# Routing eight experts from the raw residual: the router's product moved into the projection before it, and the first expert gathered alone

## The chip, the cores and the metric

The kernel runs as one program on one core of a Trainium2 chip. The metric is device time in microseconds, from the first to the last instruction and what little lies around it; of several executions the median is given. The core has a matrix engine (TensorE, "PE" in the rows, its weight loads "PEld"), a vector engine (VectorE, "DVE"), an activation engine (ScalarE, "ACT"), a general engine (GpSimd, "POOL") and a queue engine (SyncE, "SP") that issues most transfers. Matrix products land in PSUM, which has eight banks of 512 float32 columns.

## The reference, cut to what matters

Two blocks run one after the other on 256 tokens of width 1024, in float32. The last two parts of the second block matter here: a Fourier mixing layer with an output projection, which adds to the residual `x`, and a mixture of eight experts of which every token takes two.

```
x = x + gate * (fourier(norm1(x)) @ w_o + b_o)
h = rms_norm(x, norm2_g) * (1 + scale) + shift        # the experts' input
logits = h @ router                                    # (256, 8)
top_v, top_i = top_k(logits, 2)
gates = softmax(top_v)
for every token, for its two experts e:
    x += gate2 * gates[e] * ((silu(h @ w1[e]) * (h @ w3[e])) @ w2[e])
out = rms_norm(x, final_g)
```

## The kernel before, in words

**The ring of weights.** All weights come over one queue (SP) in units of 1 MB, each into a slot of a ring (`raw_unit`, line 123). In the experts' stage the ring has 16 slots: ten in the pool `ringB`, which the stages before also use, and six in `ringC`, whose memory only comes free when the Fourier projection is over. A unit is asked for as soon as the slot before it is released by the last product that reads it.

**The projection before.** `out_proj` takes `w_o` in two halves of two units. For each half it walks over two token halves `tt` and two column blocks `u`; each of these is 24 products, then two VectorE operations (lines 397 and 398) that add the result into `x`, and a ScalarE square with a sum (line 320) for the next norm. TensorE's order here is made by a planner that goes by readiness and program order.

**From the projection to the first expert.** `row_rstd` sums the squares and makes the inverse root in some ten tiny VectorE operations (lines 335 and 176 to 183). `norm_T` scales and transposes `x` in one product with a diagonal (line 363) and applies scale and shift while it copies out of PSUM, one half of a bank on VectorE (line 366), the other on ScalarE (line 368), into `mhT`. The router's product (line 1061) gives logits as rows; they are transposed, each token's two experts are found (lines 1070 to 1091), positions in each expert's list follow from two products with a triangle and with ones (1096, 1097) and three VectorE operations, and `rank_experts` sorts the experts by load. Position 0 is always expert 0, whatever its load. `mhT` is transposed back to rows `ht` (lines 1108 and 1110).

**Gather.** `gather` builds for a pair of experts a one-hot matrix from tokens to slots (line 1227) and multiplies it with `ht` (line 1234), which gives the pair's inputs, features on the partitions, in `xg`. It does so in four steps; each fills one bank with two blocks of 192 columns and copies both out in one ScalarE copy (line 1236). The first pair is gathered before the first expert. Later pairs are gathered in the last chunk of an odd expert: a step is queued as a filler and issued after each fourth of an `expert_up` half.

**The experts.** `experts_in_order` fixes TensorE's order by hand. Each expert runs seven chunks; a chunk needs six units: four for `expert_up` (w1 and w3, two halves), two for `expert_down` of the chunk before. The number of slots of 32 tokens per place is `PLACE_STRIPS = (3, 2, 3, 3, 2, 3, 3, 2)`, and TensorE's work is in proportion to it, while the bytes are the same for all.

Of the kernel before, what the change touches and what calls it, by code (L numbers as in the profile page):

```python
# [9 lines left out]
F = mybir.dt.float32  # L10
# [3 lines left out]
AF = mybir.ActivationFunctionType  # L14
OP = mybir.AluOpType
# [4 lines left out]
T = 256  # L20
KD = D // 128
# [78 lines left out]
class Kern:  # L100
# [281 lines left out]
    def out_proj(self, pool, w, yhi, ylo, targets):  # L382
# [616 lines left out]
    def fourier(self):  # L999
        nc, a, x = self.nc, self.a, self.x  # L1000
        with ExitStack() as st:
# [33 lines left out]
            self.out_proj(A, a["fnet_w_o_2"][0], fh, fl, [(self.X, g, 0)])  # L1035

    def moe(self):
        nc, tc, a, x, ct, sm = self.nc, self.tc, self.a, self.x, self.ct, self.sm
        with ExitStack() as st:
            A = self.pool(st, "MA", 1)  # L1040
            ht = A.tile([128, 2, D], F, name="ht")
            G = A.tile([128, 2, N_EXP], F, name="G")
            pos = A.tile([128, 2, N_EXP], F, name="pos")
            later = [A.tile([128, 2, N_EXP], F, name="pos%d" % i) for i in (2, 3, 4)]
            cnt = A.tile([128, 1], I32, name="cnt")
            order = A.tile([128, N_EXP], I32, name="order")
            with ExitStack() as s2:
                ps_all = self.pool(s2, "mps1", 2, psum=True)
                self.ps = ps_all
                N = self.pool(s2, "MN", 1)  # L1050
                g2 = self.gate("g_a1_2")
                hT = N.tile([128, KD, 256], F, name="mhT", bufs=1)
                rw = N.tile([128, KD, N_EXP], F, name="rw", bufs=1)
                nc.gpsimd.dma_start(rw, a["moe_router_2"][0].rearrange("(k p) e -> p k e", p=128))
                self.norm_T(N, self.X, *self.scale_cols(self.need("a1_2"), 0, self.vec["norm2"][:, 8:16]), dst_f=hT)
# [3 lines left out]
                lg = ps_all.tile([128, 512], F, tag="mm", name="mm")  # L1059
                for k in range(KD):  # L1060
                    nc.tensor.matmul(lg[0:N_EXP, :T], rw[:, k, :], hT[:, k, :], start=k == 0, stop=k == KD - 1)
                lT = N.tile([N_EXP, T], F, name="lT", bufs=1)
                nc.vector.tensor_copy(lT, lg[0:N_EXP, :T])
                lt = ps_all.tile([128, 512], F, tag="mm", name="mm")
                for tt in range(2):
                    nc.tensor.transpose(lt[:, N_EXP * tt:N_EXP * tt + N_EXP], lT[:, 128 * tt:128 * tt + 128],
                                        self.id[0:N_EXP, 0:N_EXP])
                for tt in range(2):
                    ls = sm.tile([128, N_EXP], F, tag="ls", name="ls")
                    nc.vector.tensor_copy(ls, lt[:, N_EXP * tt:N_EXP * tt + N_EXP])  # L1070
# [5 lines left out]
                    nc.vector.tensor_copy(tf, ti)  # L1076
                    e = sm.tile([128, 1], F, tag="ge", name="ge")
# [6 lines left out]
                    m1 = sm.tile([128, 8], F, tag="m1", name="m1")  # L1084
                    m2 = sm.tile([128, 8], F, tag="m2", name="m2")
                    io = ct[:, C_IO8:C_IO8 + 8]
                    nc.vector.tensor_scalar(m1, io, tf[:, 0:1], None, OP.is_equal)
                    nc.vector.tensor_scalar(m2, io, tf[:, 1:2], None, OP.is_equal)
                    nc.vector.tensor_add(M[:, tt, :], m1, m2)
# [3 lines left out]
                off = N.tile([128, 2, N_EXP], F, name="off")  # L1093
                nc.vector.tensor_scalar(off, M.bitcast(F), -1000.0, 1000.0, OP.mult, OP.add)
                pp = ps_all.tile([128, 2, 2, N_EXP], F, tag="mm", name="mm")
                nc.tensor.matmul(pp[:, 0], tri, M, start=True, stop=True)
                nc.tensor.matmul(pp[:, 1], self.ones_r, M, start=True, stop=True)
                sums = N.tile([128, 2, N_EXP], F, name="sums")
                nc.vector.tensor_copy(sums, pp[:, 1])
                nc.vector.tensor_add(pos, off, pp[:, 0])  # L1100
                nc.vector.tensor_add(pos[:, 1, :], pos[:, 1, :], sums[:, 0, :])
                nc.vector.tensor_add(sums[:, 0, :], sums[:, 0, :], sums[:, 1, :])
                self.rank_experts(N, sums[:, 0, :], pos, G, order, cnt, later)
                for tt in range(2):
                    for j in range(2):
                        tp = ps_all.tile([128, 512], F, tag="tp", name="tp")
                        for b in range(4):
                            nc.tensor.transpose(tp[:, 128 * b:128 * b + 128], hT[:, 4 * j + b, 128 * tt:128 * tt + 128], self.id)
                        js = slice(512 * j, 512 * j + 512)
                        (nc.scalar.copy, nc.vector.tensor_copy)[j](ht[:, tt, js], tp)  # L1110
# [3 lines left out]
            nc.gpsimd.tensor_scalar(self.wfin, self.wfin, -0.125, 0.0, OP.mult, OP.add)  # L1114
            self.B = self.pool(st, "MB", 2)
            more = self.pool(st, "ringC", 1)
# [3 lines left out]
            self.mh = dict(ht=ht, G=G, g2=g2, order=order)  # L1120
            self.experts(pos)
# [5 lines left out]
    def rank_experts(self, N, n, pos, G, order, cnt, later):  # L1127
# [23 lines left out]
        old = N.tile([128, 2, N_EXP], F, name="old")  # L1151
        for v in (pos, G):
            nc.vector.tensor_copy(old, v)
            for tt in range(2):
                turn(v[:, tt, :], old[:, tt, :])
        for i, p in enumerate(later):
            for tt in range(2):
                nc.vector.scalar_tensor_tensor(p[:, tt, :], cap, -float(i + 1), pos[:, tt, :], op0=OP.mult, op1=OP.add)
# [6 lines left out]
    def experts(self, pos):  # L1165

        with self.tc.manual_schedule(engines={mybir.EngineType.PE}):
            self.experts_in_order(pos)

    def experts_in_order(self, pos):  # L1170
        nch = D_FF // 512
        self.fill = []
        pairs = [None, None]
        self.gather(0, pos, pairs)
        self.filler(99)
        prev = None
        for e in range(N_EXP):
            for c in range(nch):
                if c == 0:
                    s = dict(e=e, id=self.expert_id(e), n=PLACE_STRIPS[e], **pairs[e % 2])  # L1180
# [38 lines left out]
    def gather(self, e0, pos, pairs):  # L1219

        nc, ct, B, ps, ht = self.nc, self.ct, self.B, self.mp, self.mh["ht"]
        iota = ct[:, C_IOTA:C_IOTA + SLOTS]
        n = 2 * SLOTS
        oh = B.tile([128, 2, 2, SLOTS], F, tag="oh", name="oh")
        for tt in range(2):
            for i in range(2):
                nc.vector.tensor_scalar(oh[:, tt, i, :], iota, pos[:, tt, e0 + i:e0 + i + 1], None, OP.is_equal)
        xg = B.tile([128, KD, n], F, tag="xg", name="xg")

        def step(k):  # L1230
            g = ps.tile([128, 512], F, tag="sc", name="sc", bufs=1)
            for i in range(2):
                for tt in range(2):
                    nc.tensor.matmul(g[:, n * i:n * i + n], ht[:, tt, 128 * (k + i):128 * (k + i) + 128],
                                     oh[:, tt].rearrange("p i s -> p (i s)"), start=tt == 0, stop=tt == 1)
            nc.scalar.copy(xg[:, k:k + 2, :], g[:, :2 * n].rearrange("p (k s) -> p k s", k=2))

        for k in range(0, KD, 2):
            self.fill.append(lambda k=k: step(k))
        for i in range(2):  # L1240
            pairs[i] = dict(oh=oh[:, :, i, :], xg=xg[:, :, SLOTS * i:SLOTS * i + SLOTS])
# [174 lines left out]
    def run(self):  # L1416
# [18 lines left out]
        with ExitStack() as st:  # L1435
            self.gp = self.pool(st, "gates2", 3)
            self.ring, self.ring_n = self.pool(st, "ringB", 2), (RING, 4, 4, 2048)
            self.rings, self.ring_at = [(self.ring, RING)], 0
            with ExitStack() as s2:
                self.hl = self.pool(s2, "halves", 2)  # L1440
                self.dense_ffn()
                self.ps = self.pool(s2, "ps3", 2, psum=True)
                self.fourier()
            self.moe()
# [33 lines left out]
```

## Time and profile before

| | |
|---|---|
| timed executions | 2065.04, 2073.06, 2074.27 us; median 2073.06 |
| the profiled execution | 2067.9 us, of which the span is 2065.8 |
| TensorE busy | 1945.0 us (94%) |
| VectorE busy | 814.2 us (39%) |
| ScalarE busy | 584.6 us (28%) |
| mean transfer rate over the span | 262 GB/s |

A busy time is a sum over the whole span. Matrix products are pipelined, so a busy TensorE may still wait inside. A float32 product appears as two records, a transpose as one.

### The profile page before, as it was taken

The numbers are of one execution on the slowest core, as the hardware profiler recorded it, in microseconds if no ns is written. First come the engines' busy times: TensorE is split into PE (matmuls) and PEld (weight loads), VectorE is DVE, ScalarE is ACT, GpSimd is POOL, SyncE is SP. The second block draws the span as 40 slices with busy tenths as digits, with TensorE's granted clock in tenths as the row PEclk, the third lists the DMA queues.
The fourth block names the chain that finished last, engine by engine and source line by source line (L and its number), as shares of the span: only waits on it lengthen the run. The fifth ranks groups of instructions, "written<-read, shape, count | busy, mean of one in ns | idle before, by whom it ended". The sixth has DMA issues, their size and how long they took to land. (4 is left out here: it accounts for less than half of the span.)

```text
span 2065.8 us, 49872 instructions
## 1 busy us (share of the span) xinstructions
PE 1945.0 (94%) x21993; PEld 1377.4 (67%) x21993; DVE 814.2 (39%) x2008; ACT 584.6 (28%) x1191; POOL 34.4 (2%) x43
## 2 busy tenths in 40 slices
PE   6999999988999987999979799999999989999995
PEld 3896469954889667999968565555556545655552
DVE  4794676876755475555554201110110101010112
ACT  3334463444623453444442101010101101010101
POOL 1000000000000000000021000000000000000000
PEclk9999999999999988999989899999999999999998
DMA  9567613574245504755553499999999999999995
GB/s 366 206 204 249 227 39 115 158 266 165 74 165 184 198 18 157 251 184 184 185 175 115 172 383 390 392 393 393 390 388 388 387 394 389 389 389 389 389 392 200
DMA packets 249956, 541.77 MB, mean 262 GB/s; under 512 B 9926, under 2 KB 88524, under 8 KB 241540
## 3 DMA queue, kind: packets, MB, share of 16 engines
q1 hardware_dynamic: 248448, 537.12, 71.5%
q8 instruction: 174, 2.85, 0.6%
q0 software_dynamic: 1040, 0.84, 0.3%
q10 hardware_dynamic: 244, 0.55, 0.1%
q14 instruction: 50, 0.41, 0.1%
HBM read 537.38 MB, written 1.10 MB: 261 GB/s over the span
## 5 line engine op out<-in xcount | busy, mean ns | idle before, releaser
L1265 PE MATMUL ha<-raw,xg 128*32 128x256 f32 x7168 | 461.5, 382 | 15.7 <-DMA raw<-in_moe_w_dram 15.7
L1265 PEld LDWEIGHTS ha<-raw,xg 128*32 128x32 f32 x7168 | 226.1, 110 | 184.7 <-issue 23.3
L1290 DVE TENSOR_TENSOR es<-es,ha 64x512 f32<-64x512 f32 x56 | 38.7, 691 | 670.6 <-ACT es L1289 670.6
L141 DVE TENSOR_TENSOR lo<-raw,hi 128x1024 fp32r<-128x1024 f32 (+2 forms) x176 | 214.6, 1226 | 178.6 <-ACT hi L140 178.2
L140 ACT CAST hi<-raw 128x1024 fp32r<-128x1024 f32 (+2 forms) x180 | 187.7, 1051 | 183.0 <-PE acc L153 65.8
L1265 PE MATMUL ya<-raw,gt 128*32 128x256 f32 x3584 | 224.1, 379 | 1.3 <-DMA raw<-in_moe_w_dram 0.6
L1265 PE MATMUL hb<-raw,xg 128*32 128x256 f32 x2240 | 176.6, 380 | 0.0
L1265 PEld LDWEIGHTS ya<-raw,gt 128*32 128x32 f32 x3584 | 117.3, 110 | 78.2 <-DMA raw<-in_moe_w_dram 1.5
L1300 ACT COPY gt<-tp 128x384 f32<-128x384 f32 (+1 forms) x56 | 24.6, 439 | 408.7 <-PE tp L1298 400.4
L151 PE MATMUL h<-fhh,hi 128*128 128x256 f32 x448 | 124.2, 285 | 0.9 <-ACT h L368 0.9
L152 PE MATMUL h<-fhl,hi 128*128 128x256 f32 x448 | 124.3, 285 | 0.0
L153 PE MATMUL h<-fhh,lo 128*128 128x256 f32 x448 | 122.6, 285 | 0.0
L1265 PEld LDWEIGHTS hb<-raw,xg 128*32 128x32 f32 x2240 | 74.6, 110 | 48.7 <-issue 0.6
L1289 ACT ACTIVATE es<-ha 64x512 f32<-64x512 f32 x56 | 33.0, 589 | 254.3 <-PE ha L1265 254.3
L151 PE MATMUL mm<-hi,dhh 128*128 128x256 f32 x320 | 90.3, 283 | 0.0
L153 PE MATMUL mm<-hi,dhl 128*128 128x256 f32 x320 | 89.8, 281 | 0.0
L152 PE MATMUL mm<-lo,dhh 128*128 128x256 f32 x320 | 89.4, 280 | 0.0
L261 PE MATMUL modps<-mraw,s 128*32 128x512 f32 x512 | 78.8, 610 | 10.7 <-DMA mraw<-in_ada_w_dram 10.7
L151 PEld LDWEIGHTS h<-fhh,hi 128*128 128x128 f32 x448 | 85.9, 194 | 2.7 <-ACT h L368 1.2
L152 PEld LDWEIGHTS h<-fhl,hi 128*128 128x128 f32 x448 | 86.0, 194 | 0.9
L1265 PE MATMUL yb<-raw,gt 128*32 128x256 f32 x1120 | 86.1, 379 | 0.0
L153 PEld LDWEIGHTS h<-fhh,lo 128*128 128x128 f32 x448 | 85.0, 194 | 0.7
(434 smaller groups left out, 3415.8 us busy)
## 6 DMA issues: line engine op xcount, KB each, us to landing
raw<-in_moe_w_dram SPq DMA_DIRECT2D x336, 1024.0 KB
mraw<-in_ada_w_dram SPq DMA_DIRECT2D x48, 1024.0 KB
raw<-in_ff_w_dram SPq DMA_DIRECT2D x42, 1024.0 KB
raw<-in_w_in_dram SPq DMA_DIRECT2D x14, 1024.0 KB
raw<-in_attn_w_qkv_dram SPq DMA_DIRECT2D x12, 1024.0 KB
m<-in_w_mod_dram SPq DMA_DIRECT2D x8, 1024.0 KB
mraw<-in_w_mod_dram SPq DMA_DIRECT2D x16, 512.0 KB
mraw<-in_w_mod_dram SPq DMA_DIRECT2D x8, 1024.0 KB
```

Of the source, the lines that this page charges most:

```text
L140: nc.scalar.copy(hi[:, :n], v)
L141: eng.tensor_sub(lo[:, :n], v, hi[:, :n].bitcast(F))
L151: mm(ps, lh, rh, start=first, stop=False)
L152: mm(ps, lh, rl, start=False, stop=False)
L153: mm(ps, ll, rh, start=False, stop=last)
L261: nc.tensor.matmul(ps[32 * j:32 * j + 32, :], stat[:, k, :], raw[:, 512 * j:512 * j + 512], start=k == 0, stop=k == KD - 1)
L1265: self.nc.tensor.matmul(out[32 * q:32 * q + 32, :], x(t), w, start=first and t != 1, stop=last, skip_group_check=True)
L1289: nc.scalar.activation(v, b[0:64, :c1 - c0], AF.Silu)
L1290: nc.vector.tensor_mul(v, v, b[64:128, :c1 - c0])
L1300: nc.scalar.copy(g.rearrange("p b h s -> p (b h s)")[:, :128 * n], t[:, :128 * n])
```

## The change

The router's product is taken from `x` itself. With `a` and `b` the columns of scale and shift, `h = x * rstd * a + b`, so the logits are `rstd * (x @ (a * router)) + b @ router`. `router_begin` loads the router's weights on GpSimd's queue ahead of the projection and prepares `a * router` and `b @ router`. After each half of `out_proj`, `router_part` transposes that half's columns of `x`, copies them out of PSUM and multiplies them with `a * router` into two banks of their own. After the projection, the logits are one VectorE operation per token half. The rows that are gathered are now `x * rstd` (one ScalarE operation per token half); scale and shift are applied when a gathered block is copied out of PSUM, so each feature block has a copy of its own. The first expert is gathered alone, with a one-hot matrix made before the ranking, and the others as pairs (1, 2), (3, 4), (5, 6) and 7 alone, in the last chunk of an even expert. The ranking writes into new tiles. `ringC` is opened ahead of the other pools, on the ground where the halves of the projection's weights lay.

```diff
     def out_proj(self, pool, w, yhi, ylo, targets, after=None):
...
+            if after:
+                after(u0)
...
+            self.router_begin()
+            self.out_proj(A, a["fnet_w_o_2"][0], fh, fl, [(self.X, g, 0)], self.router_part)
+
+    def router_begin(self):
...
+        nc.gpsimd.dma_start(rw, a["moe_router_2"][0].rearrange("(k p) e -> p k e", p=128))
+        self.rt_ab = self.scale_cols(self.need("a1_2"), 0, self.vec["norm2"][:, 8:16])
...
+        nc.vector.tensor_mul(self.rwa, rw, ac[:, :, None].to_broadcast(shape))
...
+        nc.tensor.matmul(ps[:, :N_EXP], self.ones, sb, start=True, stop=True)
...
+    def router_part(self, u0):
+
+        nc = self.nc
+        for u in (u0, u0 + 1):
+            tp = self.ps.tile([128, 2, 256], F, tag="tp", name="tp")
+            for t in range(2):
+                for i in range(2):
+                    k = 2 * u + i
+                    nc.tensor.transpose(tp[:, i, 128 * t:128 * t + 128], self.x[:, t, 128 * k:128 * k + 128], self.id)
+            for t in range(2):
+                ts = slice(128 * t, 128 * t + 128)
+                (nc.vector.tensor_copy, nc.scalar.copy)[t](self.xT[:, 2 * u:2 * u + 2, ts], tp[:, :, ts])
+                for k in (2 * u, 2 * u + 1):
+                    nc.tensor.matmul(self.lg[t][:, :N_EXP], self.xT[:, k, ts], self.rwa[:, k, :],
+                                     start=k == 0, stop=k == KD - 1)
...
+            more = self.pool(st, "ringC", 1)
             A = self.pool(st, "MA", 1)
...
-                self.norm_T(N, self.X, *self.scale_cols(self.need("a1_2"), 0, self.vec["norm2"][:, 8:16]), dst_f=hT)
...
+                rs = [self.row_rstd(self.X, tt) for tt in range(2)]
+                es = []
                 for tt in range(2):
                     ls = sm.tile([128, N_EXP], F, tag="ls", name="ls")
-                    nc.vector.tensor_copy(ls, lt[:, N_EXP * tt:N_EXP * tt + N_EXP])
+                    nc.vector.scalar_tensor_tensor(ls, self.lg[tt][:, :N_EXP], rs[tt], self.lb, op0=OP.mult, op1=OP.add)
+                    nc.scalar.activation(ht[:, tt, :], x[:, tt, :], AF.Copy, scale=rs[tt])
...
+                first = self.onehot(A, "first", pos, 0, 1)
...
+                self.rank_experts(N, sums[:, 0, :], (pos, posp), (G, Gp), order, cnt, later)
-                for tt in range(2):
-                    for j in range(2):
-                        tp = ps_all.tile([128, 512], F, tag="tp", name="tp")
...
-        self.gather(0, pos, pairs)
+        self.gather(0, 1, pos, pairs, first)
...
-                if c == nch - 1 and e % 2 and e + 1 < N_EXP:
-                    self.gather(e + 1, pos, pairs)
+                if c == nch - 1 and e % 2 == 0 and e + 1 < N_EXP:
+                    self.gather(e + 1, min(2, N_EXP - 1 - e), pos, pairs)
...
+        kn = 4 if begin else 2
+
+        def step(k0):
+            g = self.mp.tile([128, 512], F, tag="h%s" % "ab"[k0 // 4] if begin else "sc", name="sc", bufs=2 if begin else 1)
+            for i in range(kn):
                 for tt in range(2):
...
+                k, v = k0 + i, g[:, n * i:n * i + n]
+                if begin and i % 2:
+                    nc.vector.tensor_scalar(xg[:, k, :], v, ac[:, k:k + 1], bc[:, k:k + 1], OP.mult, OP.add)
+                else:
+                    nc.scalar.activation(xg[:, k, :], v, AF.Identity, bias=bc[:, k:k + 1], scale=ac[:, k:k + 1])
```

## Rows read from the trace of the kernel before

**Rows 1.** Stretches: length; PE, PEld, DVE, ACT, POOL busy (count); PE clock; DMA share; GB/s.

```profile
1123.50:1142.50 19.00, 14.58 (x66) 8.66 (x66) 7.93 (x34) 5.00 (x9) 1.28 (x2) 0.82 0.91 331
1142.50:1170.30 27.80, 18.25 (x142) 13.47 (x146) 8.20 (x61) 3.72 (x8) 0.00 (x0) 0.63 0.01 3
...
1195.00:1285.00 90.00, 90.00 (x1640) 53.92 (x1632) 5.85 (x11) 7.75 (x17) 0.00 (x0) 1.00 1.03 387
1285.00:1363.00 78.00, 78.00 (x1246) 45.45 (x1241) 11.89 (x23) 10.20 (x23) 0.00 (x0) 1.00 1.04 393
...
1600.00:1720.00 120.00, 111.04 (x1812) 61.91 (x1808) 15.38 (x29) 12.08 (x28) 0.00 (x0) 0.97 1.04 391
1720.00:2031.00 311.00, 304.31 (x5134) 175.80 (x5126) 35.36 (x65) 31.00 (x71) 0.00 (x0) 1.00 1.04 389
```

**Rows 2.** SP's instructions in order of time: start, duration, instruction.

```profile
1169.93 0.93 SPq L123 DMA_DIRECT2D raw<-in_moe_w_dram  x2
...
1224.46 0.37 SPq L123 DMA_DIRECT2D raw<-in_moe_w_dram  x1
1229.61 0.37 SPq L123 DMA_DIRECT2D raw<-in_moe_w_dram  x1
```

**Rows 3.** Timeline from the projection's last product: start, duration, instruction, [idle before, releaser].

```profile
1123.17 0.28 PE L153 MATMUL mm<-hi,fl 128*128 128x256 f32 x1
...
1123.95 0.47 DVE L398 TENSOR_TENSOR x<-x,gt 128x256 f32<-128x256 f32 x1
...
1126.94 0.16 DVE L183 SCALAR_TENSOR_TENSOR ry<-ru,ry 128x1 f32<-128x1 f32 x1
...
1127.57 1.19 PE L363 MATMUL tp<-dr,x 128*128 128x128 f32 x4 [1.99 <-DVE dr L355]
1128.38 0.99 DVE L366 TENSOR_SCALAR mhT<-tp,acol,fm_a 128x256 f32<-128x256 f32 x2 [0.95 <-PE tp L363]
...
1128.97 1.22 PE L363 MATMUL tp<-dr,x 128*128 128x128 f32 x4 [0.21 <-DVE mhT L366]
```

**Rows 4.** Timeline of VectorE, from the logits to the one-hot matrix.

```profile
1141.06 0.24 DVE L1070 COPY ls<-mm 128x8 f32<-128x8 f32 x2
...
1143.71 0.15 DVE L1089 TENSOR_TENSOR M<-m,m 128x8 fp32r<-128x8 f32 x1
...
1144.83 0.17 DVE L1101 TENSOR_TENSOR pos<-pos,sums 128x8 f32<-128x8 f32 x1
...
1149.87 1.52 DVE L1227 TENSOR_SCALAR oh<-ct,pos 128x96 f32<-128x96 f32 x8
```

**Rows 5.** Timeline of TensorE, the first gather and the first expert.

```profile
1150.58 2.90 PE L1234 MATMUL sc<-oh,ht 128*128 128x192 f32 x8 [6.21 <-DVE oh L1227]
1154.16 2.93 PE L1234 MATMUL sc<-oh,ht 128*128 128x192 f32 x8 [0.69 <-ACT xg L1236]
...
1164.02 1.56 PE L1265 MATMUL ha<-raw,xg 128*32 128x256 f32 x16
```

**Rows 6.** Timeline of TensorE's weight loads, at the low and at the full clock.

```profile
1131.08 1.78 PEld L363 LDWEIGHTS tp<-dr,x 128*128 128x128 f32 x8 [0.85 <-issue]
...
1136.99 0.52 PEld L363 LDWEIGHTS tp<-dr,x 128*128 128x128 f32 x4 [0.43 <-issue]
```

**Rows 7.** Timeline of TensorE, one step of a later gather among an expert's products.

```profile
1585.87 1.57 PE L1234 MATMUL sc<-oh,ht 128*128 128x192 f32 x8
1587.37 1.07 PE L1265 MATMUL ha<-raw,xg 128*32 128x256 f32 x16
```

**Rows 8.** ScalarE's groups of one shape, 1115 to 1165 us: busy, mean ns.

```profile
L368 ACT ACTIVATE mhT<-tp,fm_a,acol 128x256 f32<-128x256 f32 x4 | 2.3, 565 | 11.0 <-PE tp L363 11.0
...
L1236 ACT COPY xg<-sc 128x384 f32<-128x384 f32 x4 | 1.9, 479 | 19.7 <-PE sc L1234 19.7
...
L1110 ACT COPY ht<-tp 128x512 f32<-128x512 f32 x2 | 1.2, 586 | 1.9 <-PE tp L1108 1.9
```

**Rows 9.** Busy time by stretch, the first gather (columns as in the first group).

```profile
1150.50:1164.00 13.50, 11.59 (x32) 9.69 (x32) 0.90 (x5) 1.44 (x3) 0.00 (x0) 0.50 0.00 0
```

More of the change, by code (lines that the diff above doesn't have):

```diff
@@ L1046, in moe @@
             order = A.tile([128, N_EXP], I32, name="order")
+            g2 = self.gate("g_a1_2")
             with ExitStack() as s2:
[L1048 to L1054, printed above, removed]
-                self.norm_T(N, self.X, *self.scale_cols(self.need("a1_2"), 0, self.vec["norm2"][:, 8:16]), dst_f=hT)
+                N = self.pool(s2, "MN", 1, side="right")
                 M = N.tile([128, 2, N_EXP], R, name="M", bufs=1)
@@ L1076, in moe @@
                     nc.vector.tensor_copy(tf, ti)
+                    m1 = sm.tile([128, 8], F, tag="m1", name="m1")
+                    m2 = sm.tile([128, 8], F, tag="m2", name="m2")
+                    io = ct[:, C_IO8:C_IO8 + 8]
+                    nc.vector.tensor_scalar(m1, io, tf[:, 0:1], None, OP.is_equal)
+                    nc.vector.tensor_scalar(m2, io, tf[:, 1:2], None, OP.is_equal)
+                    nc.vector.tensor_add(M[:, tt, :], m1, m2)
+                    es.append((tv, m1, m2))
+                off = N.tile([128, 2, N_EXP], F, name="off")
+                nc.vector.tensor_scalar(off, M.bitcast(F), -1000.0, 1000.0, OP.mult, OP.add)
+                pp = self.ps.tile([128, 2, 2, N_EXP], F, tag="mm", name="mm", bufs=4)
+                nc.tensor.matmul(pp[:, 0], tri, M, start=True, stop=True)
+                nc.tensor.matmul(pp[:, 1], self.ones_r, M, start=True, stop=True)
+                sums = N.tile([128, 2, N_EXP], F, name="sums")
+                nc.vector.tensor_copy(sums, pp[:, 1])
+                nc.vector.tensor_add(pos, off, pp[:, 0])
+                nc.vector.tensor_add(pos[:, 1, :], pos[:, 1, :], sums[:, 0, :])
+                first = self.onehot(A, "first", pos, 0, 1)
+                for tt, (tv, m1, m2) in enumerate(es):
                     e = sm.tile([128, 1], F, tag="ge", name="ge")
@@ L1114, in moe @@
             nc.gpsimd.tensor_scalar(self.wfin, self.wfin, -0.125, 0.0, OP.mult, OP.add)
+            self.router_close()
             self.B = self.pool(st, "MB", 2)
-            more = self.pool(st, "ringC", 1)
             self.rings = [(self.ring, RING)] * RING + [(more, RING_MORE)] * RING_MORE
@@ L1119, in moe @@
             self.mp = self.pool(st, "mps2", 2, psum=True)
-            self.mh = dict(ht=ht, G=G, g2=g2, order=order)
-            self.experts(pos)
+            self.mh = dict(ht=ht, G=Gp, g2=g2, order=order)
+            self.experts(posp, first)
             cr = nc.values_load(cnt[0:1, 0:1], min_val=0, max_val=2 * T)
@@ L1150, in rank_experts @@
         turn(nr, n)
-        old = N.tile([128, 2, N_EXP], F, name="old")
-        for v in (pos, G):
-            nc.vector.tensor_copy(old, v)
+        for old, new in (pos, G):
             for tt in range(2):
-                turn(v[:, tt, :], old[:, tt, :])
+                turn(new[:, tt, :], old[:, tt, :])
         for i, p in enumerate(later):
             for tt in range(2):
-                nc.vector.scalar_tensor_tensor(p[:, tt, :], cap, -float(i + 1), pos[:, tt, :], op0=OP.mult, op1=OP.add)
+                nc.vector.scalar_tensor_tensor(p[:, tt, :], cap, -float(i + 1), pos[1][:, tt, :], op0=OP.mult, op1=OP.add)
         nc.vector.tensor_sub(nr, nr, cap)
@@ L1217, in filler, with onehot @@
             n -= 1
[L1219 to L1224, printed above, removed]
-        for tt in range(2):
[L1226 to L1232, printed above, removed]
+    def onehot(self, pool, tag, pos, e0, m):
+        iota = self.ct[:, C_IOTA:C_IOTA + SLOTS]
+        oh = pool.tile([128, 2, 2, SLOTS], F, tag=tag, name=tag)[:, :, 0:m, :]
+        for tt in range(2):
+            for i in range(m):
+                self.nc.vector.tensor_scalar(oh[:, tt, i, :], iota, pos[:, tt, e0 + i:e0 + i + 1], None, OP.is_equal)
+        return oh
@@ new lines, in gather @@
+    def gather(self, e0, m, pos, pairs, oh=None):
+        nc, B, ht = self.nc, self.B, self.mh["ht"]
+        ac, bc = self.rt_ab
+        n = m * SLOTS
+        begin = e0 == 0
+        if oh is None:
+            oh = self.onehot(B, "oh", pos, e0, m)
+        xg = B.tile([128, KD, 2 * SLOTS], F, tag="xg", name="xg")[:, :, 0:n]
+        kn = 4 if begin else 2
+        def step(k0):
+            g = self.mp.tile([128, 512], F, tag="h%s" % "ab"[k0 // 4] if begin else "sc", name="sc", bufs=2 if begin else 1)
+            for i in range(kn):
@@ L1233, in step @@
                 for tt in range(2):
-                    nc.tensor.matmul(g[:, n * i:n * i + n], ht[:, tt, 128 * (k + i):128 * (k + i) + 128],
+                    nc.tensor.matmul(g[:, n * i:n * i + n], ht[:, tt, 128 * (k0 + i):128 * (k0 + i) + 128],
                                      oh[:, tt].rearrange("p i s -> p (i s)"), start=tt == 0, stop=tt == 1)
-            nc.scalar.copy(xg[:, k:k + 2, :], g[:, :2 * n].rearrange("p (k s) -> p k s", k=2))
-        for k in range(0, KD, 2):
+                k, v = k0 + i, g[:, n * i:n * i + n]
@@ L1438, in run @@
             self.rings, self.ring_at = [(self.ring, RING)], 0
+            sp = ExitStack()
+            self.RT = self.pool(sp, "RT", 1, side="right")
             with ExitStack() as s2:
```

69 lines of the change are left out of this document (28 added, 41 removed).

## The prediction

> **What bounds the kernel now.** I read the page first: TensorE is busy almost throughout, which doesn't say what it waits for inside. The second view is busy time by stretch [rows 1]. From 1195 us to 2031 us the queue moves 387 to 393 GB/s whatever TensorE does, and between 1600 and 1720 TensorE stands idle for 9 us, so the experts' stage is bound by its 336 units of 1 MB. At 393 GB/s a unit takes 1.0486 MB / 393 GB/s = 2.67 us. The end of the kernel is therefore the sum of the times in which the queue moves and of those in which it doesn't. One large gap is there to be had: from 1142.5 to 1170.3 us it moves 3 GB/s [rows 1]. The reader should see why: all 16 slots are full, and none comes free until the first expert has used one, at 1169.93 [rows 2], 5.9 us after that expert's first product at 1164.02 [rows 5].
>
> The third view is the timeline between. The projection's last product starts at 1123.17 [rows 3], the first gather's at 1150.58 and the first expert's at 1164.02 [rows 5]: 27.4 us for norm, router and ranking, and 13.4 us for the gather, which runs at half clock throughout [rows 9].
>
> The fourth is SP's order of issue within expert 0 (three strips). Per chunk two units leave at the end of each half of `expert_up` and two during `expert_down`. The last of these goes at 1224.46, the next at 1229.61 [rows 2], 5.15 us later, the longest pause of the chunk. A chunk's six units take 6 x 2.67 = 16.0 us; 387 against 393 GB/s [rows 1] leaves 1.5% of that, 0.24 us per chunk, without a transfer, and I place it at the end of this pause. So TensorE and the queue are almost level with three strips, and the queue keeps no reserve. So within expert 0, with the ring full, each microsecond that TensorE gets more to do is a microsecond in which the queue stands. In expert 1 (two strips, 1285 to 1363) the queue runs flat out at 393 while TensorE draws on the ring; later experts live on what is left of that lead, and it is used up by 1600 to 1720 [rows 1]. There, and at the end, more work on TensorE is hidden.
>
> **The change, part by part.** All against the profiled execution, 2067.9 us.
>
> *Router inside the projection.* Per block `u` there are four transposes and four products of a 128-column weight with 8 moving columns, eight records. At full clock four weight loads take 0.52 us [rows 6], 0.13 each; the moving side is short, so 4 x 0.13 + 8 x 0.13 = 1.6 us per block. Two of the four blocks fall ahead of the projection's last product, which TensorE runs without a gap: +3.2 us, and I add 0.8 for the bias product and for waits where a transpose stands in TensorE's queue and `x` is late. Its DMA (32 KB on GpSimd's queue) and the five small VectorE operations lie beside the projection's first half; without that cover they would cost some 5 us.
>
> *From the projection to the first gather.* After the last product, `x` is final 1.25 us later (1123.95 + 0.47), and the inverse root is there at 1127.10 (1126.94 + 0.16), 3.93 us after that product [rows 3]. The last two blocks' transposes, copies and products, 3.2 us of TensorE and two copies of about half a microsecond, run beside that chain; I let them delay it by 0.4. From the logits on the rows of before hold: from 1141.06 to the choice M at 1143.86 (1143.71 + 0.15) is 2.8 us, of which about 0.8 were the copy of `ht` and gate arithmetic that now come later, so 2.0; M to the positions is 1.14 (1144.83 + 0.17 less 1143.86); the first one-hot column needs about 0.35 [rows 4]. The sum is 4.0 + 3.93 + 0.4 + 2.0 + 1.14 + 0.35 = 11.8 us after 1123.17. The first gather starts at 1135.0 instead of 1150.58: 15.6 us gained. The bounds are 13 (blocks in TensorE's queue that wait for `x`) and 17.
>
> *The first gather.* It has 32 records as before, each of half the columns. The loads bind: 1.78 us for eight at low clock [rows 6], 0.22 each, so 32 x 0.22 = 7.0 us if nothing interrupts. But now four feature blocks lie in one bank, each with a copy of its own. The rows show what happens then: `norm_T` does the same, and its second half's products began at 1128.97, as soon as VectorE had read the first half of that bank, at the releaser "DVE mhT" [rows 3]. The Trainium skill says the same (PSUM — Partial Sum Buffer, section Terms): two engines on one bank at once are a collision, so accesses have to be kept apart. By that rule the sum ends at the 2059.4 below, without it at rival 1's 2052, and this trace agrees with the rule. Per block: four records start within 0.66 us; the copy starts 0.59 after the last (1128.38 against a second record at 1127.57 + 0.22) [rows 3]; the copy of 96 columns takes 0.43 (565 ns for 256 columns, less 160 columns at the 0.84 ns that 586 for 512 and 479 for 384 give) [rows 8]; 0.05 to restart. Behind the waiting products TensorE has the rest of the gather and the first expert, and SP waits for that expert's first release. That is 1.73 us on six blocks, and 0.88 on the two after which the bank changes: 12.1, or 11.7 with the odd copies on VectorE a little shorter. The clock was low during the whole of the first gather before, with TensorE occupied 86% of it [rows 9]; the new one has longer gaps and follows a pause of about 4 us, so I take it low. Against 13.4 that is a gain of 1.7; the bounds are 6.4 (no waits) and -3 (the odd copies queue behind the 7 us of ranking on VectorE). The first expert starts near 1146.7 instead of 1164.0: 17.3 us gained. The six units of `ringC` took 19 us at 331 GB/s [rows 1]; shifted by 3 to 4 us they land by 1146, ahead of the first release near 1152.6, so the queue doesn't cap that.
>
> *The gather in expert 0.* Before, experts 0 and 1 were gathered up front and the next pair in expert 1, whose two strips hide it. Now the pair (1, 2) comes in the last chunk of expert 0, where nothing hides it. A step took 1587.37 - 1585.87 = 1.50 us at full clock [rows 7], 0.19 a record; four steps 6.0. With a copy per block, the second block waits within the step: 4 x 0.19 + 0.33 + 0.05 + 0.51 (ScalarE, 192 columns, by the same slope) + 0.05 before it [rows 8], less what overlaps, and 0.76 after it: 2.2 us, four steps 8.8. The release at the end of that half is late by as much, and the queue, which has nothing left then, stands for as long. Bounds: 0 (the queue has a reserve that I don't see) and 9.5. The gathers in experts 2, 4 and 6 are paid from the lead, which the rows show spent only at 1600 to 1720 and again before 2031: nothing.
>
> **The sum.** 15.6 + 1.7 - 8.8 = 8.5 us gained: 2067.9 - 8.5 = 2059.4 for an execution like the profiled one. The median of the runs shown is 5.2 us above that execution and the fastest 2.9 below; I take half of the 5.2 and predict 2062 us.
>
> **The rivals.** (1) *No wait inside a bank*: then the first gather takes 7.0 and expert 0's 6.0: 15.6 + 6.4 - 6.0 = 16 us gained, 2052 for the profiled execution, 2054 with the same half step. Against it stands the releaser in [rows 3]; for it, that TensorE's order is made by hand in the experts. (2) *The queue has a reserve in expert 0*, so that the gather there is free: 17.3 gained, 2051, or 2053 with the half step. The little the queue loses per chunk (387 against 393) speaks against it. (3) *The ranking stands in front of the odd copies on VectorE*, up to 4.7 us: 3.8 gained, 2064, or 2067. Before, VectorE slipped later work into the ranking's pauses, so I hold it for less likely. (4) *The other side*: TensorE's queue stalls inside the projection, because a block's transposes are queued ahead of products that could run and wait for `x`, while VectorE is occupied with splitting the next weights. If each of the first three blocks stalls for more than 2.8 us, all is gone; at 4.5 us (two additions of 0.45, two splits of 1.2, a copy of 0.4, and the hand-overs) it is 5 us slower, 2073, or 2076 with the half step. TensorE had no gap there before, and the planner goes by readiness, which speaks against it. (5) The change does what it says, since every new product replaces one that stood on the path; that the path gets no shorter I exclude.
>
> **Chances.** The forecast 0.52, of which a quarter reaches a gain over 0.5%; rivals 1 and 2 together 0.27; rival 3 0.14; rival 4 0.07. A measurement of this kernel can tell about 0.5% from no change, 10.4 us of 2073. Faster by more than that: 0.13 + 0.27 = 0.40; within 0.5%: 0.39 + 0.14 = 0.53; slower: 0.07, counted whole. The range runs from 2049 (rivals 1 and 2 against the lowest of the times shown, 2065.04) to 2070 (rival 3 against the median, 2073.06); the forecast's own is 2055 to 2068.
>
> **What would show it.** The first gather's records start 11 to 13 us after the projection's last product. In the first gather groups of four records stand 1.6 to 1.8 us apart, each with ScalarE or VectorE as releaser, at clock 0.50; if they run through, rival 1 holds. In expert 0's last chunk steps of 2.2 us appear, and the transfer rate there drops for some 8 us; if it stays at 387, rival 2 holds. The gap of the queue ahead of the first release shrinks from 27.8 us to about 8. TensorE inside the projection shows no waits; if it does, rival 4. The prediction is wrong if the queue is not what the end hangs on, that is if TensorE doesn't run dry at the end of the last expert.

## The result and the profile after

The changed kernel takes 2079.56 us, median of 10 runs (2069.32 to 2084.98); the kernel before, in 10 runs, 2067.10 (2062.76 to 2074.27). The ratio is 1.0057, 95% interval 1.0040 to 1.0074: about 12 us slower. The profiled execution has a span of 2076.5 us, against 2065.8.

Three stretches show where the 10.7 us between the spans arise. This is the timeline of the changed kernel, at the first product of the Fourier stage's norm, at the projection's last product, through the first gather, and where the queue starts to move again.

```profile
1082.49 1.91 PE L363 MATMUL tp<-dr,x 128*128 128x128 f32 x6 [10.96 <-DVE dr L355]
...
1138.01 0.29 PE L153 MATMUL mm<-hi,fl 128*128 128x256 f32 x1
...
1146.40 1.14 PE L1266 MATMUL sc<-first,ht 128*128 128x96 f32 x4 [0.77 <-PE mm L1118]
1151.73 1.17 PE L1266 MATMUL sc<-first,ht 128*128 128x96 f32 x4 [4.19 <-ACT xg L1272]
1153.45 1.17 PE L1266 MATMUL sc<-first,ht 128*128 128x96 f32 x4 [0.54 <-DVE xg L1270]
...
1162.19 1.08 PE L1301 MATMUL ha<-raw,xg 128*32 128x256 f32 x8
...
1151.25 0.43 ACT L1272 ACTIVATE xg<-sc,fm_a,acol 128x96 f32<-128x96 f32 x1 [6.82 <-DVE Gp L1169]
...
1169.98 0.92 SPq L123 DMA_DIRECT2D raw<-in_moe_w_dram  x2
...
1254.30 2.96 SPq L123 DMA_DIRECT2D raw<-in_moe_w_dram  x2
...
1269.55 0.99 SPq L123 DMA_DIRECT2D raw<-in_moe_w_dram  x2
```

And busy time by stretch, with the columns of [rows 1]:

```profile
1146.00:1162.00 16.00, 8.76 (x32) 7.34 (x32) 7.29 (x43) 2.67 (x5) 0.00 (x0) 0.50 0.65 249
1162.00:1170.00 8.00, 8.00 (x106) 3.96 (x109) 0.38 (x1) 0.34 (x1) 0.00 (x0) 0.69 0.01 2
...
1240.00:1260.00 20.00, 19.40 (x336) 11.66 (x329) 1.03 (x2) 1.85 (x4) 0.00 (x0) 1.00 1.04 390
1260.00:1280.00 20.00, 18.19 (x250) 11.07 (x252) 1.03 (x2) 4.92 (x10) 0.00 (x0) 1.00 0.58 206
```

What to see. First, the Fourier stage, which the change leaves alone up to its projection, begins at 1082.49; before, the same row stands at 1070.29 (shown with e1 below). So 12.2 us are gone before the first changed line is due. Second, between that row and the first freed slot, 12.15 us are won back: 1169.98 less 1082.49 is 87.49, before 1169.93 [rows 2] less 1070.29, 99.64. The queue restarts at the same instant in both kernels. Third, the queue then issues nothing from 1257.3 (1254.30 + 2.96) to 1269.55, and its rate falls to 206 GB/s in a stretch for which [rows 1] had 387. From the restart to the end of the span are 906.5 us, before 895.9: 10.6 more, and that is the whole difference. Of this, 9.0 us are there when the queue asks for its last unit, 864.9 us after the restart and before 855.9 (rows below the table of the experiments).

The first of the three was in nobody's account. This is the kernel before, where the attention's first softmax begins (VectorE's last split of the values' weights, the first maximum, TensorE's scores):

```profile
700.91 1.23 DVE L141 TENSOR_TENSOR lo<-raw,hi 128x1024 fp32r<-128x1024 f32 x1 [0.44 <-ACT hi L140]
702.47 0.69 DVE L891 TENSOR_REDUCE am<-S 128x1 f32<-128x512 f32 x1 [0.33 <-PE S L887]
...
701.31 1.99 PE L887 MATMUL S<-dk,dq 64*128 64x512 f32 x8
704.22 1.12 PE L887 MATMUL S<-dk,dq 64*128 64x512 f32 x2 [0.92 <-ACT P L895]
...
710.00:720.00 10.00, 10.00 (x52) 4.25 (x49) 7.96 (x23) 5.80 (x18) 0.00 (x0) 1.00 0.34 140
```

and this the changed one:

```profile
698.67 0.96 POOL L1045 DMA_DIRECT2D rw<-in_moe_router_dram  x1 [40.86 <-ACT dv L831]
...
699.48 1.23 DVE L141 TENSOR_TENSOR lo<-raw,hi 128x1024 fp32r<-128x1024 f32 x1 [0.44 <-ACT hi L140]
704.94 0.22 DVE L1052 TENSOR_TENSOR rwb<-rw,fm_a 128x64 f32<-128x64 f32 x1 [4.23 <-DMA rw<-in_moe_router_dram]
705.08 0.68 DVE L893 TENSOR_REDUCE am<-S 128x1 f32<-128x512 f32 x1
...
699.88 1.99 PE L889 MATMUL S<-dk,dq 64*128 64x512 f32 x8
706.86 2.86 PE L889 MATMUL S<-dk,dq 64*128 64x512 f32 x4 [5.00 <-ACT P L897]
...
710.00:720.00 10.00, 10.00 (x26) 2.41 (x18) 5.22 (x15) 3.42 (x9) 0.00 (x0) 0.50 0.39 118
```

`router_begin` is written ahead of the Fourier projection, but the scheduler has put its `rwb` some 400 us earlier, in front of the first softmax on VectorE. Its input is loaded only from 698.67 on, when the last copy of the attention's values releases the place, and lands six microseconds later. VectorE stands for 4.23 us in front of `rwb`, and the first maximum starts 4.37 us after the split's end, where it had been 0.33; ScalarE waits for VectorE, TensorE for ScalarE, 5.00 us; and the granted clock of the next 10 us is 0.50 (1.2 GHz) where it had been 1.00 (2.4 GHz).

### The profile page after: what moved, and what is told of

Read it like the earlier page. It is cut to its first block, busy times and chain, and to the rows that moved or that the text cites. A ratio compares the mean times of both kernels' runs of the same rounds, so it can differ in the third digit from the quotient of the medians.

```text
span 2076.5 us, 49935 instructions
## 1 busy us (share of the span) xinstructions
PE 1949.1 (94%) x22009; PEld 1378.6 (66%) x22009; DVE 814.0 (39%) x2009; ACT 594.7 (29%) x1211; POOL 34.5 (2%) x43
## 5 line engine op out<-in xcount | busy, mean ns | idle before, releaser
L141 DVE TENSOR_TENSOR lo<-raw,hi 128x1024 fp32r<-128x1024 f32 (+2 forms) x176 | 214.4, 1225 | 178.5 <-ACT hi L140 177.3
```

What stands on the lines that cost most here:

```text
L141: eng.tensor_sub(lo[:, :n], v, hi[:, :n].bitcast(F))
```

## The experiments

Nine kernels ran. For each, three stretches of its profiled execution: from the end of VectorE's last split of the values' weights (L141 near 700 us, start plus 1.23) to the Fourier norm's first product (L363); from there to the first freed slot's load (SP); and from there to the end of the span. The column after the third has the part of the third up to the queue's last load of a unit. All in us.

| kernel | split to Fourier | Fourier to queue | queue to end | of it, to the last load | median | ratio to before (95%) |
|---|---|---|---|---|---|---|
| before | 368.2 | 99.6 | 895.9 | 855.9 | 2067.10 | 1 |
| after | 381.8 | 87.5 | 906.5 | 864.9 | 2079.56 | 1.0057 (1.0040 to 1.0074) |
| e1 | 374.1 | 98.7 | 896.1 | 856.0 | 2076.52 | 1.0049 (1.0030 to 1.0067) |
| e2 | 367.2 | 84.0 | 907.4 | 864.9 | 2066.60 | 1.0004 (0.9990 to 1.0017) |
| e3 | 379.9 | 86.7 | 904.2 | 861.6 | 2074.31 | 1.0029 (1.0010 to 1.0048) |
| e4 | 381.8 | 84.7 | 906.0 | 862.7 | 2077.68 | 1.0044 (1.0025 to 1.0063) |
| e5 | 368.0 | 87.6 | 903.6 | 860.3 | 2064.11 | 0.9986 (0.9973 to 0.9999) |
| e6 | 368.2 | 83.9 | 906.9 | 864.7 | 2064.02 | 0.9988 (0.9975 to 1.0000) |
| e7 | 368.8 | 73.9 | 905.3 | 865.0 | 2054.71 | 0.9939 (0.9918 to 0.9959) |
| e8 | 369.6 | 73.7 | 901.7 | 859.8 | 2052.54 | 0.9923 (0.9906 to 0.9941) |
| e9 | 369.1 | 79.3 | 898.6 | 857.1 | 2052.93 | 0.9922 (0.9894 to 0.9950) |

The last load is read from rows like these, of the kernel before, the changed one and e4:

```profile
2025.82 1.01 SPq L123 DMA_DIRECT2D raw<-in_moe_w_dram  x1
...
2034.87 1.02 SPq L123 DMA_DIRECT2D raw<-in_moe_w_dram  x1
...
2033.73 1.03 SPq L123 DMA_DIRECT2D raw<-in_moe_w_dram  x1
```

What lies ahead of the first column takes between 700.7 us (after) and 708.7 (e8), 702.1 before, so the spans themselves don't compare to a few us; the 12.2 us above are the 13.6 of the first column less the 1.4 by which the changed kernel's split ended sooner. The middle column varies by up to 3.6 us between kernels whose code there is the same (after, e2 to e5), so differences of that size in it need a row of their own. The variation is in the Fourier stage: from its norm's first product to the projection's first it takes 27.3 us (e2) to 30.0 (e5), while the projection takes 25.7 in every kernel with the router in it, and 23.1 before and in e1. Behind the last load another 39.9 to 43.3 us follow, 42.5 in e2 and 40.3 in e7, whose code there is the same; so the third column alone is sharp to some 2 us. The kernel before had medians of 2066.05 beside e1 to e4, 2064.98 beside e5 to e8 and 2068.62 beside e9.

**e1, the hoisted load alone.** The kernel before, with `RT` and `router_begin` and nothing that uses them:

```diff
+            sp = ExitStack()
+            self.RT = self.pool(sp, "RT", 1, side="right")
...
+            self.router_begin()
             self.out_proj(A, a["fnet_w_o_2"][0], fh, fl, [(self.X, g, 0)])
```

> The kernel before, with one thing of the change alone: the router's weights are loaded and scaled (and the row of ones times them taken) where the change does it, from a pool opened ahead of the dense layer; nobody uses the results. Theory A (a load that waits for the attention's memory): the scheduler puts rwb ahead of the attention's first softmax on VectorE, rwb waits some 4 us for its load near 705 us, TensorE stands about 5 us behind it, its granted clock is 0.50 in the stretch after, and all from the Fourier stage on lies 12 us later: 2079 us. Theory B (the 12.2 us come from the rest of the change, for example from where memory lies later on): no such wait, 2067 us. Theory C (only the wait itself counts and the clock would have fallen anyway): 4 to 5 us, 2072 us.

2076.52 us, ratio 1.0049: 6 to 14 us slower by the interval. Its timeline, and one stretch of it:

```profile
702.23 0.96 POOL L1043 DMA_DIRECT2D rw<-in_moe_router_dram  x1 [40.86 <-ACT dv L829]
...
708.52 0.23 DVE L1050 TENSOR_TENSOR rwb<-rw,fm_a 128x64 f32<-128x64 f32 x1 [4.26 <-DMA rw<-in_moe_router_dram]
...
710.45 2.07 PE L887 MATMUL S<-dk,dq 64*128 64x512 f32 x3 [5.03 <-ACT P L895]
...
710.00:720.00 10.00, 9.55 (x32) 2.96 (x33) 8.81 (x27) 5.55 (x15) 0.00 (x0) 0.76 0.38 117
```

Same wait, same 5.03 us of TensorE, and later columns of the table as in the kernel before. For the comparison, the Fourier stage's first product in the kernel before:

```profile
1070.29 2.12 PE L363 MATMUL tp<-dr,x 128*128 128x128 f32 x7 [10.96 <-DVE dr L355]
```

Theory B falls, and the interval leaves C's 4 to 5 us out. In this one profile the first stretch is 5.9 us longer, though, not 13.6 as in the changed kernel's, with the same wait in both. The rows that differ are the clock's: 0.76 against 0.50 in 710 to 720. The attention's maxima (`am`) show where the delay arises. In the four profiles with the early load (after, e1, e3, e4) the first of them starts 4.0 to 4.1 us later behind the split than before. At the tenth the delay is 11.0, 5.4, 11.2 and 11.0 us, and the granted clock from the first to the tenth is 0.56, 0.78, 0.56 and 0.56, where the kernel before has 1.00. So the wait costs 4 us in every execution seen, and most of the rest arises behind it, within 20 us, while the clock is low.

**e2, the load without its wait.** The changed kernel with the load at the kernel's start, into memory of its own:

```diff
-        rw = M.tile([128, KD, N_EXP], F, name="rw")
-        nc.gpsimd.dma_start(rw, a["moe_router_2"][0].rearrange("(k p) e -> p k e", p=128))
+        rw = self.rw
...
+        self.rw = self.cp.tile([128, KD, N_EXP], F, name="rw")
+        nc.gpsimd.dma_start(self.rw, a["moe_router_2"][0].rearrange("(k p) e -> p k e", p=128))
```

> The changed kernel, with the router's weights loaded at the start of the kernel into memory that nobody else uses, so that rwb, which stays in front of the attention's first softmax, has nothing to wait for. Theory A: no wait at 705 us, the Fourier stage starts 12.2 us sooner, and since the queue stands idle ahead of the first expert all of it comes through: 2067 to 2068 us. Theory B: nothing moves, 2079.5 us. Theory C: 4 to 5 us come back, 2075 us.

2066.60 us, ratio 1.0004. `rwb` stays ahead of the softmax and waits for nothing:

```profile
701.65 0.22 DVE L1051 TENSOR_TENSOR rwb<-rw,fm_a 128x64 f32<-128x64 f32 x1
...
702.18 1.23 DVE L141 TENSOR_TENSOR lo<-raw,hi 128x1024 fp32r<-128x1024 f32 x1
703.73 0.69 DVE L893 TENSOR_REDUCE am<-S 128x1 f32<-128x512 f32 x1 [0.33 <-PE S L889]
...
1132.00 1.14 PE L1265 MATMUL sc<-first,ht 128*128 128x96 f32 x4 [0.77 <-PE mm L1117]
...
1147.74 1.94 PE L1300 MATMUL ha<-raw,xg 128*32 128x256 f32 x16
...
1154.63 0.92 SPq L123 DMA_DIRECT2D raw<-in_moe_w_dram  x2
```

So theory A holds from both sides: adding the early load to the kernel before costs what taking its wait from the changed kernel gives back. It also lays bare the rest of the change: the first expert starts 16.3 us earlier than in [rows 5] and the queue 15.3 us earlier than in [rows 2], and the median is no better than before. Of the 15.6 us that the middle column wins, the third gives 11.5 back (907.4 against 895.9).

**e3 and e4, the gather inside expert 0.** In the changed kernel, with the hoisted load still in, e3 takes one feature block per step; e4 gathers only expert 1 in expert 0 and puts the pairs where the kernel before has them:

```diff
-        kn = 4 if begin else 2
+        kn = 4 if begin else 1
```

```diff
-                if c == nch - 1 and e % 2 == 0 and e + 1 < N_EXP:
-                    self.gather(e + 1, min(2, N_EXP - 1 - e), pos, pairs)
+                if c == nch - 1 and e + 1 < N_EXP and e + 1 not in pairs:
+                    self.gather(e + 1, 2 if e else 1, pos, pairs)
```

> The changed kernel, with one feature block in each step of a gather inside an expert (eight steps instead of four, spread over both halves of the chunk), so that no product waits for the copy of the block before it out of the same bank. In the trace of the changed kernel a step took 2.5 us: two products pairs of 0.92 and a wait of 0.60. Theory D (the columns are the cost): 4 x 0.6 = 2.4 us come back, 2077 us. Theory E (the waits of the four steps and what they set off at the queue are the cost, as the prediction had it in part): most of the 10 us lost there come back, 2070 us.

> The changed kernel, with only expert 1 gathered in expert 0's last chunk (96 columns instead of 192), and the pairs (2,3), (4,5), (6,7) in the last chunks of experts 1, 3 and 5, where the kernel before has them. Theory D: about half of the loss in expert 0 comes back and the pairs cost nothing, as in the kernel before, since the queue has a reserve by then: about 5 us, 2074.5 us. Theory E (steps and waits, not columns): four steps stay, at most 1 us comes back, 2078.5 us. Theory F (a pair in expert 1 costs as much as in expert 0): no gain or slower, 2080 us or above.

TensorE's timeline of a step in the changed kernel:

```profile
1258.05 0.92 PE L1266 MATMUL sc<-oh,ht 128*128 128x192 f32 x4
1259.57 0.92 PE L1266 MATMUL sc<-oh,ht 128*128 128x192 f32 x4 [0.60 <-ACT xg L1272]
...
1261.85 0.92 PE L1266 MATMUL sc<-oh,ht 128*128 128x192 f32 x4
```

in e3:

```profile
1260.43 0.92 PE L1266 MATMUL sc<-oh,ht 128*128 128x192 f32 x4
...
1262.71 0.92 PE L1266 MATMUL sc<-oh,ht 128*128 128x192 f32 x4
```

and in e4:

```profile
1259.10 0.69 PE L1266 MATMUL sc<-oh,ht 128*128 128x96 f32 x4
1260.31 0.69 PE L1266 MATMUL sc<-oh,ht 128*128 128x96 f32 x4 [0.52 <-ACT xg L1272]
...
1262.36 0.69 PE L1266 MATMUL sc<-oh,ht 128*128 128x96 f32 x4
```

Without steps a feature block of the expert takes 1.30 us there. With one it takes 3.80 in the changed kernel (1261.85 less 1258.05), so four steps cost 10.0; in e3 2.28 (1262.71 less 1260.43), so eight cost 7.8. The table's third column follows: 906.5 and 904.2. For e3 theory D holds, 2.3 of the expected 2.4 us, and 3.3 by the last load; its median is lower than that by some 3 us, inside the intervals. For e4 D's "half" was wrong: four records of 96 columns take 0.69 us, four of 192 take 0.92, so halving the columns takes a quarter off. With a block e4's step takes 3.26 (1262.36 less 1259.10), so its four cost 7.8, 2.2 less than in the changed kernel, and by the last load the queue is 2.2 us less late (862.7, 864.9): theory D's cause, in half its size, and more than E's 1 us. The third column and the median show less of it, 0.5 and 1.9 us; behind the last load e4's profile takes 1.7 us more, less than the 2.1 between e2 and e7. The pair that now lies in expert 1 shows no fall of the rate there, so theory F falls.

**e5 to e8, the repairs on top of e2.** e5 is e2 with the edits of e3 and e4. e6 is e2 with the ranking's tiles in the pool that outlives the gather. e7 is e6 with each feature block of the first gather in a bank of its own (four banks in turn) and all its copies on ScalarE. e8 is all of them.

```diff
-                N = self.pool(s2, "MN", 1, side="right")
+                N = A
...
-        kn = 4 if begin else 2
+        kn = 1 if begin else 2
...
-            g = self.mp.tile([128, 512], F, tag="h%s" % "ab"[k0 // 4] if begin else "sc", name="sc", bufs=2 if begin else 1)
+            g = self.mp.tile([128, 512], F, tag="h%s" % "ab"[k0 % 2] if begin else "sc", name="sc", bufs=2 if begin else 1)
...
-                if begin and i % 2:
+                if False:
```

> The kernel of e2 (router's weights loaded at the start, 2066.6 us) with both edits of e3 and e4: only expert 1 is gathered in expert 0's last chunk, and each step takes one feature block, so that no product waits for a copy. Theory D (TensorE's time in the steps is the cost, paid because the queue has no reserve in expert 0): 8 steps of 0.6 us instead of 4 of 2.5 us, the queue's loss around 1250 to 1270 us falls from 9.4 us in e2 to 4 or 5, 2062 us. Theory E2 (the pause of the queue is set by something else than the steps): a loss of 8 to 9 us stays, 2066 us.

> The kernel of e2 with the ranking's tiles put into the pool that stays open through the experts, so that xg no longer lies on memory that the ranking still uses. Theory G (the first copy waits for that memory): the first gather's first copy starts at 1133.3 instead of 1136.8 us, that is 1.3 us after its product instead of 4.8; the copies on VectorE still stand behind parts of the ranking; 2 to 3.5 us come through: 2063.5 us. Theory H (it is the order on VectorE that holds the gather): the second copy waits as before, nothing is gained, 2066.5 us.

> The kernel of e6, and in the first gather each feature block gets a bank of its own out of four, and all eight copies run on ScalarE. Theory G with bank waits: eight blocks of 0.6 us each at the low clock and a last copy, 1132.0 to 1138 us instead of 1147.7, 10 us come through: 2057 us. Theory I (the queue's idle time ahead of the first expert is nearly used up, and after it TensorE, not the first product, sets the pace): half of it or less comes through, 2062 us. Theory H: at most 1 us, 2066 us.

> The kernel of e7 with e5's steps: all four repairs. If the parts add (theories A, D, G): 2066.6 less 10 less 5, 2052 us, 0.7% faster than before. If theory I holds: 2058 us. If neither the steps nor the first gather is worth anything: 2066 us.

e5: 2064.11 us, and 903.6 in the third column against e2's 907.4. By the last load the queue is 4.4 us behind the kernel before, where e2 was 9.0 behind, and 4 or 5 had been expected: theory D. e6: 2064.02. Its rows:

```profile
1137.60 1.14 PE L1265 MATMUL sc<-first,ht 128*128 128x96 f32 x4 [0.82 <-DVE first L1247]
1139.27 1.17 PE L1265 MATMUL sc<-first,ht 128*128 128x96 f32 x4 [0.52 <-ACT xg L1271]
...
1149.73 0.66 PE L1300 MATMUL ha<-raw,xg 128*32 128x256 f32 x4
...
1138.78 0.43 ACT L1271 ACTIVATE xg<-sc,fm_a,acol 128x96 f32<-128x96 f32 x1 [3.16 <-PE sc L1265]
```

The first copy now starts 1.18 us after its product, in e2 4.8, and the first gather takes 12.1 us (1149.73 less 1137.60) instead of 15.7: theory G for the first copy; H falls. This rests on the rows: the median's 2.6 us are within the intervals of e2 and e6, and the middle column shows nothing (83.9, 84.0), because in e6's profile the Fourier stage takes 2.6 us more than in e2's and the first expert 0.9 more up to its first release. What is left are the waits inside the banks. e7 takes them away:

```profile
1135.59 6.33 PE L1265 MATMUL sc<-first,ht 128*128 128x96 f32 x32 [0.82 <-DVE first L1247]
1141.85 1.07 PE L1300 MATMUL ha<-raw,xg 128*32 128x256 f32 x16
...
1135.00:1142.00 7.00, 6.41 (x36) 6.34 (x40) 6.12 (x41) 3.06 (x8) 0.00 (x0) 0.58 1.05 393
1240.00:1260.00 20.00, 18.19 (x267) 11.17 (x270) 1.03 (x2) 4.40 (x9) 0.00 (x0) 1.00 0.57 209
```

All 32 records run through in 6.3 us, and the table's middle column is 10 us shorter than e2's (73.9, 84.0): 2054.71 us, 12 below e2 where 10 were expected; theory G holds, I falls. What the banks did and what the one engine for the copies did isn't separated. e8 adds e5's steps and ends at 2052.54, ratio 0.9923, as the sum of the parts had it.

**e9, the first expert not gathered apart.** e7 with the pairing of the kernel before:

```diff
-        self.gather(0, 1, pos, pairs, first)
+        self.gather(0, 2, pos, pairs)
...
-                if c == nch - 1 and e % 2 == 0 and e + 1 < N_EXP:
+                if c == nch - 1 and e % 2 and e + 1 < N_EXP:
```

> The kernel of e7 (2054.7 us) with the pairing of the kernel before: experts 0 and 1 are gathered together from the ranked positions ahead of the first expert, and the next pairs in the last chunks of experts 1, 3 and 5. If what the first expert gains by being gathered apart is given back in expert 0, because the queue has no reserve there (my reading of the traces): the first gather waits for the ranking (about 4.5 us) and its 192 columns take some 3 to 4 us more, and the 9 us that the queue of e7 loses around 1250 us come back: within 2 us of e7, 2053 to 2056 us. If gathering it apart is a gain of its own: 2060 us or above. If the pair in expert 0 cost more than the queue's pause shows: 2050 us or below.

2052.93 us, ratio 0.9922:

```profile
1138.97 0.98 PE L1264 MATMUL sc<-oh,ht 128*128 128x192 f32 x2 [4.59 <-DVE oh L1246]
1140.12 7.17 PE L1264 MATMUL sc<-oh,ht 128*128 128x192 f32 x30 [0.17 <-DVE oh L1246]
1147.21 1.07 PE L1299 MATMUL ha<-raw,xg 128*32 128x256 f32 x16
...
1240.00:1260.00 20.00, 20.00 (x364) 11.96 (x360) 1.03 (x2) 1.61 (x4) 0.00 (x0) 1.00 1.04 388
```

The first expert starts 5.4 us later than in e7, the queue restarts 5.4 later by the table's middle column, and the third column is 6.7 shorter (7.9 by the last load), with no pause at 1250 us. Gathering the first expert apart is worth nothing here: what it wins in front is paid in expert 0. Which of e8 and e9 is better these runs don't settle; both beat both kernels, by about 0.8% and 1.3%.

## Why the prediction was wrong

Forecast 2062.0 us, range 2049 to 2070; measured 2079.56. Set against the profiled execution, by the prediction's own steps:

| step | predicted | changed kernel | where |
|---|---|---|---|
| ahead of the Fourier stage | 0 | +12.2 | 1082.49 less 1070.29 |
| router inside the projection | +4.0 | +2.6 | 25.70 less 23.10, the projection's first to its last product |
| that product to the first gather | -19.6 | -19.0 | 8.39, from 27.41 |
| first gather | -1.7 | +2.4 | 15.79, from 13.44 |
| first expert to first freed slot | 0 | +1.9 | 7.79, from 5.91 |
| gather in expert 0 | +8.8 | +9.0 | 864.9 less 855.9, first freed slot to last load |
| behind the last load | 0 | +1.7 | 41.6 less 39.9 |
| sum, rounded | -8.5 | +10.7 | |

(27.41 is 1150.58 less 1123.17 in [rows 3] and [rows 5]; the predicted -19.6 is 11.8 less the 4.0 of the row above, less 27.41. So by its own sum the gather had to start 7.8 us after the projection's last product; the sign "11 to 13 us" has those 4.0 in it by mistake, and 8.4 were measured.)

**The failed step** is a sentence of *Router inside the projection*: that the router's DMA and its five small VectorE operations "lie beside the projection's first half; without that cover they would cost some 5 us". They did not lie there. The memory of `RT` comes free in the attention, the scheduler takes what is ready, and the cover was looked for in the wrong stage: where `rwb` was put, nothing covered its wait. The wait itself was the right size (4.23 us, and 5.00 of TensorE); what followed on it, some 20 us at a lower clock, and that all of it passes through, since the queue stands idle later, were missing. The Trainium skill says of VectorE's queue that it is strict first in, first out (PSUM — Partial Sum Buffer, section Engine vs sequencer instructions); the trace agrees, with the first maximum 4.0 us late behind a waiting product. This was a way to the other side, and the rival named for that side was another one: between the projection's first and last product TensorE waits for nothing, and the router's records there cost 2.6 us, so rival 4 did not happen.

**Mis-sized: the first gather.** The waits inside a bank are as predicted: records 1.7 us apart, ScalarE and VectorE as releasers at 0.52 to 0.54, clock 0.50. The 12.1 us of e6 are the predicted 11.7. Missing was the ranking, 3.6 us, and by another way than rival 3's: the even copy on ScalarE waited, because `xg` lies where the ranking's last tile had to be done first, and e6 frees it by giving the ranking other memory. Rival 1 is refuted by the same rows; e7 shows that it was a gain to be had, not one that the change took.

**Expert 0: the right loss from a step that was too short.** Rival 2 is refuted: there is no reserve. A step took 2.5 us where 2.2 were predicted, and the four 10.0 instead of 8.8; the terms that the prediction lists for a step add up to 2.46, and the 0.26 that it took off as "what overlaps" stood on no row. The queue is 9.9 us late at the request that follows the steps (1277.75 less 1169.98, before 1267.82 less 1169.93) and 9.0 at its last, because it gets 0.9 back in expert 1; so it is partly luck that 9.0 lies so near to 8.8. The mechanism held: e3, e4, e5 and e9 shorten or remove the steps, and the last load comes sooner after the restart with them (by 3.3, 2.2, 4.6 and 7.9 us).

**Mis-sized: the release.** The first expert's products were taken at the pace of before. In the changed kernel the clock is 0.69 over 1162 to 1170, after 16 us in which TensorE was busy 8.8. In e7, with TensorE busy in 6.4 of 7 us ahead of it, the expert starts at full clock (1.00 over 1141 to 1147) and frees a slot after 5.4 us (1147.26 less 1141.85).

Without the delay ahead, e2's profile is 3.8 us shorter than before's and its ratio is 0.9990 to 1.0017, so the forecast of 8.5 would have been too high as well. In the changed kernel TensorE did run dry at the end, as the forecast needed: the experts' waits for weights come to 9.7 us, 3.5 of them behind 2000 us, and the mean rate from 1280 to 2031 us is 391 GB/s.

**Open.** Of the first column's 13.6 us, 4.0 are the wait and 7.0 more arise by the tenth maximum, at a clock of 0.56; how much of these is the clock alone, and what makes the 2.6 behind them, was not separated. e1's profile has 5.9 in all for the same wait; why its clock stayed higher no run shows. That it is memory that holds the router's load back is read from the releaser (`dv`) and from e2, where other memory and an earlier place in the queue came together. Of the 2.7 us that e9's third column has over the kernel before, 1.2 are there by the last load and the rest behind it; neither is explained, nor are the 1.7 behind the changed kernel's last load.

## What to carry to other kernels

An operation that is moved or made independent can be pulled by the scheduler across whole stages, as far as its inputs and its memory let it: before costing it at nothing, ask what is the earliest place at which it could stand in its engine's queue, and what is behind it there if its input is late. A load of 32 KB, issued where its landing had no slack, cost more than everything that the change won.

Where transfers bound the kernel, a gain in front counts only until the next place where the ring has no reserve; price the two together, as e9 does. And where several small results share a PSUM bank, each with its own copy, give them banks of their own first: with all copies on one engine, that was 6 us in one gather of eight blocks (e6 to e7).

## What was not expected of the hardware

Records of 96 columns are not half as long as those of 192: 0.69 against 0.92 us for four in expert 0. The weight loads between them have the same 128 columns in both.

Filling TensorE's gaps did more than remove them. The same 32 records took 15.8 us in the changed kernel, 3.6 of them the ranking's, at a granted clock of 0.50; 12.1 us in e6 with the waits inside the banks alone; and 6.3 us in e7 without either, at 0.58. The expert behind them in e7 then began at 1.07 us for 16 records, where the changed kernel needed 1.08 us for 8.
